# Second feed-forward of a two-layer diffusion backbone: gate and up matmuls with operands in two scaled fp16 parts

## The chip, the cores and the metric

The kernel runs on one NeuronCore of a Trainium2 chip. The time is the device time of one launch in microseconds (us). TensorE (PE in the profile) does matmuls, VectorE (DVE) and ScalarE (ACT) elementwise work, GpSimd (POOL) and SyncE (SP) mostly issue DMA transfers; each engine works through its own instructions in order and waits on semaphores for the others.

## The reference, cut to what matters

Two layers work on 1024 latent tokens and 256 context tokens with 1024 channels. Layer 0 mixes with Fourier and Hyena branches, layer 1 with neighbourhood attention. Each layer ends in a modulated SwiGLU feed-forward of width 2816:

```python
def swiglu(u, w_gate, w_up, w_down):
    return (jax.nn.silu(u @ w_gate) * (u @ w_up)) @ w_down
...
h_lat = h_lat + g2 * swiglu(modulate(rms_norm(h_lat, norm2_g[i]), sh2, sc2),
                            ffn_w_gate[i], ffn_w_up[i], ffn_w_down[i])
```

`sh2`, `sc2` and `g2` are columns per channel, made from the conditioning vector by a matrix product with `ada_w`. All inputs are float32.

## The kernel before

Channels lie on the 128 partitions, tokens along the free dimension. To keep float32 accuracy every operand of a large product is split in two parts: `hi` is the value rounded to fp32r (a reduced float32 that PE takes at a high rate), `lo` is what is left, also in fp32r. A product is three matmuls, hi x hi, hi x lo and lo x hi, into the same PSUM bank. The split is one cast on ScalarE (L349) and one subtraction on VectorE (L351), both in `split`.

The feed-forward `ffn` runs once per layer. Gate and up go through 11 iterations; iteration i takes two rows of 128 output channels of each matrix and computes them by Strassen-Winograd's scheme for 2x2 blocks: seven block products instead of eight. `wino_weights` loads two weight rows of 128x1024, and makes the sums S1 to S4 of their quarters on VectorE (L1866 to L1874) and the split parts of A11, A12, A22 and S1 to S4. `wino_steps` issues the products. A product is 4 blocks x 3 = 12 matmuls of 128x512 (`prod`, L1888), so gate and up of an iteration are 2 x 7 x 12 = 168 and a layer's are 1848. Products that share a PSUM bank follow each other, and ScalarE copies the bank's sum out between them (`snap`, L1893), so that PE may only go on in that bank behind the copy. The other side, the blocks B and T of the normed input (`self.X`, 28 pairs of hi and lo), is made in `wino_first` and `wino_second` (L1779 is a `lo` there). `finish` (L1982 and on) multiplies silu(gate) by up and POOL stores seven blocks for `down`, the third matrix (L2065), which keeps fp32r in both layers.

Between the two layers run `values` (the value projection of layer 1) and the attention. The first layer's stage also computes the modulation columns of layer 1: `ada_group` loads 128x1024 pieces of `ada_w` over the POOL queue (L336 in `ldr`) and reduces them on VectorE (L561), three pieces per iteration. Ahead of layer 1's iterations, `wino_begin` starts five half products (120 matmuls), while the norm of its input is still being worked out (`rms_begin`, with a square root at L604; `rms_end`, L615).

Tiles come from pools with a fixed number of buffers: `S4` (128x1024 float32, 21 buffers), `S2` (128x512, 35), `G` (4), `T`, `TK`, `ws`/`wh`/`wl` for weights. A scheduler that estimates times puts the program's instructions in a fixed order on each engine, and a load into a buffer waits until the buffer's last user is done. `with self.follow(ins)` binds an instruction behind another.

Of the kernel before, what the change touches and what calls it, by code (L numbers as in the profile page):

```python
# [258 lines left out]
class Builder:  # L259
    def __init__(self, ctx, tc, a, out, taps=None, stop=None):  # L260
# [17 lines left out]
        self.banks = 8  # L278
        self.sq = {}

    def pad(self, pool, w):
# [1462 lines left out]
    def pair(self, key, wide):  # L1744

        if wide:
            t = self.S4(F32R)
            t = (t[:, :512], t[:, 512:])
        else:
            t = (self.S2(F32R), self.S2(F32R))  # L1750
        self.X[key] = t
        return t

    def wino_first(self, h, l, m, r):

        nc = self.nc
        self.X, self.raw = {}, {}
        for j in range(4):
            for b in (j, j + 4):
# [4 lines left out]
                nc.scalar.activation(hi, t, AF.Identity, bias=sh)  # L1764
                nc.vector.scalar_tensor_tensor(lo, t, sh, hi.bitcast(F32), op0=ADD, op1=SUB)
                self.raw[b] = t
                yield

    def wino_second(self, h, l, m, r):
# [6 lines left out]
        def out(key, j, src):  # L1776
            hi, lo = self.pair((key, j), l == 1 or len(self.X) < 17)
            nc.scalar.copy(hi, src)
            los.append(nc.vector.tensor_tensor(lo, src, hi.bitcast(F32), SUB).ins)  # L1779

# [42 lines left out]
        for j in range(4):  # L1823
# [3 lines left out]
            nc.scalar.activation(hi, t22, AF.Identity, bias=sh)  # L1827
            nc.vector.scalar_tensor_tensor(lo, t22, sh, hi.bitcast(F32), op0=ADD, op1=SUB)
            yield

    def wino_first_row(self, src, wide):

        wh, wl = self.weights(src, wide=wide)
        return {"A11": (wh[:, :512], wl[:, :512]), "A12": (wh[:, 512:], wl[:, 512:])}

    def wino_weights(self, src, done=None, half=None):

# [14 lines left out]
        w = {} if done is None else done  # L1852
        if done is None:
            wh = self.W("wh", "wh", F32R)
# [4 lines left out]

        def op(key, x):  # L1860
            hi, lo = self.T(F32R) if key == "S4" else self.S2(F32R), self.S2(F32R)
            self.split(x, hi, lo)
            w[key] = (hi, lo)

# [56 lines left out]
    def wino_pair(self, l, i, m, done=None, half=None):  # L1921
        w = self.a[("gate", "up")[m]]
        return self.wino_weights([w[l, 2 * i], w[l, 2 * i + 1]], done, half)

    def wino_begin(self, l, i, m, tile, ctile=None, wide=True):

        w = self.wino_first_row(self.a[("gate", "up")[m]][l, 2 * i], wide)
        s = Steps(self.wino_steps(w, tile, ctile))
# [4 lines left out]
    def ffn(self, l, u, h, hs, second, after, keep=None, begun={}):  # L1933
# [24 lines left out]
        if u is not None:  # L1958
            for fb in range(NFB):
# [10 lines left out]
                if fb >= 2:  # L1970
# [22 lines left out]
        for i in range(NFB // 2):  # L1993
# [20 lines left out]
            for k in (3, 4, 5) if i == 0 and l == 1 else ():  # L2014
                g.to(k)
                up.to(k)
            g.to(5)
            up.to(1)
            g.to(7)
            gate = dict(self.res)  # L2020
            for k in ((0, 0), (1, 1), (0, 1)):
                nc.scalar.activation(gate[k], gate[k], AF.Silu)
            t = self.G()
            nc.scalar.activation(t, gate[(1, 0)], AF.Silu)
# [11 lines left out]
            for _ in range(3 if i < 8 else 2):  # L2036
                next(todo, None)
        prev[0].to(7)
        finish(n2 - 1, prev[1])
# [443 lines left out]
    def run(self):  # L2483
# [372 lines left out]
```

## Time and profile before

| | |
|---|---|
| runs, median of 3 | 2882.15 us (2878.31 to 2882.6) |
| the profiled execution, its span | 2876.0 us |
| its gate and up matmuls of layer 0, starts (L1888) | 902.7 to 1322.8 us |
| its gate and up matmuls of layer 1, starts (L1888) | 2222.9 to 2656.0 us |
| HBM traffic over the span | 183 GB/s |

The profiled execution has a span but no time of its own from outside; the median of the runs is 6.15 us above the span. In the profile, a line such as `L1888 PE MATMUL ps<-s,s 128*128 128x512 f32` names the source line, the engine, the operation, output and inputs, the weights' and the output's shape and the type (fp32r shows as f32 for matmuls). `PEld` is the load of the weights into the array, which overlaps the matmul before. In a timeline, "x30" is a run of 30 such instructions, with the start of the first, the time until the end of the last, and in brackets how long the engine idled before and what released it. A matmul's own duration includes its latency; its rate is read from the number of matmuls in a stretch.

### The profile page before, as it was taken

To read this page: it belongs to the slowest core of one execution; us is meant where nothing else is said; L and a number is where in the kernel's file an instruction comes from. 1 tells how busy PE (TensorE), PEld (TensorE's weight loads), DVE (VectorE), ACT (ScalarE), POOL (GpSimd) and SP (SyncE) were. 2 spreads that over 40 slices of the span, in tenths; PEclk is the share of its full clock that TensorE was granted. 3 is DMA by queue.
4 is the path that set the end of the run, shared out by engine and by line. 5 is a ranking of instruction groups with operands and counts; after the bars stand their busy time and mean duration, and the time that the engine had idled before them with its cause. 6 is when DMAs were issued, how large, how long until landed. Compare 5 with 4: busy or idle time off the path is not lost. (4 is left out here: it accounts for less than half of the span.)

```text
span 2876.0 us, 43758 instructions
## 1 busy us (share of the span) xinstructions
PE 2777.6 (97%) x15570; PEld 2330.9 (81%) x15570; DVE 2089.7 (73%) x3653; ACT 1318.9 (46%) x2267; POOL 539.9 (19%) x873
## 2 busy tenths in 40 slices
PE   7999889999999999999999999999999999999998
PEld 3877677788899888888888888888887788888887
DVE  5678788768777888967777536777777987664556
ACT  3434225543554333333445426777764533333434
POOL 1210234351001112212010002232222022112000
PEclk9999999999999999999999999999999999999999
DMA  7355536756556555659885436777866376434763
GB/s 261 104 161 174 179 117 209 231 171 232 204 184 210 198 198 196 221 183 336 302 307 167 147 116 154 194 180 187 233 211 221 101 254 225 149 110 166 230 195 134
DMA packets 298600, 557.35 MB, mean 194 GB/s; under 512 B 82056, under 2 KB 128842, under 8 KB 298382
## 3 DMA queue, kind: packets, MB, share of 16 engines
q1 hardware_dynamic: 234894, 367.34, 41.2%
q0 software_dynamic: 60640, 182.50, 18.1%
q10 hardware_dynamic: 2848, 4.72, 0.4%
q8 instruction: 123, 2.02, 0.3%
q14 instruction: 95, 0.78, 0.1%
HBM read 407.10 MB, written 119.80 MB: 183 GB/s over the span
## 5 line engine op out<-in xcount | busy, mean ns | idle before, releaser
L1888 PE MATMUL ps<-s,s 128*128 128x512 f32 x1976 | 488.1, 390 | 1.1 <-ACT g L1893 1.1
L1888 PEld LDWEIGHTS ps<-s,s 128*128 128x128 f32 x1976 | 370.9, 188 | 78.9 <-ACT g L1893 1.5
L345 PE MATMUL ps<-s,wh 128*128 128x256 f32 (+1 forms) x1784 | 412.9, 334 | 4.0 <-DVE s L786 1.8
L345 PEld LDWEIGHTS ps<-s,wh 128*128 128x128 f32 x1784 | 299.0, 190 | 39.2 <-DVE s L786 2.3
L345 PE MATMUL ps<-s,wl 128*128 128x256 f32 (+1 forms) x892 | 273.5, 332 | 2.0 <-DVE wl L351 2.0
L349 ACT CAST s<-s 128x1024 fp32r<-128x1024 f32 (+2 forms) x192 | 172.4, 926 | 197.3 <-DMA s<-d 171.5
L2065 PE MATMUL ps<-s,s 128*128 128x512 f32 (+1 forms) x1000 | 259.8, 383 | 3.2 <-DVE s L351 3.1
L351 DVE TENSOR_TENSOR wl<-ws,wh 128x1024 fp32r<-128x1024 f32 (+1 forms) x141 | 168.9, 1200 | 123.8 <-ACT wh L349 119.2
L345 PE MATMUL pq<-s,wh 128*128 128x512 f32 (+1 forms) x840 | 256.1, 385 | 0.6 <-DVE s L897 0.6
L345 PE MATMUL ps<-s,s 128*128 128x65 f16 (+4 forms) x2748 | 229.2, 235 | 16.1 <-DMA s<-tk 9.0
L349 ACT CAST wh<-ws 128x1024 fp32r<-128x1024 f32 (+1 forms) x141 | 144.4, 1026 | 202.3 <-PE ps L345 87.9
L349 ACT CAST s<-t 128x512 fp32r<-128x512 f32 (+2 forms) x238 | 133.9, 583 | 224.6 <-PE ps L1888 76.2
L351 DVE TENSOR_TENSOR s<-s,s 128x1024 fp32r<-128x1024 f32 (+2 forms) x170 | 190.6, 1154 | 58.2 <-ACT s L349 58.0
L2065 PEld LDWEIGHTS ps<-s,s 128*128 128x128 f32 x1000 | 184.5, 188 | 41.2 <-DVE s L351 4.9
L351 DVE TENSOR_TENSOR s<-t,s 128x512 fp32r<-128x512 f32 (+2 forms) x238 | 150.9, 649 | 76.7 <-ACT s L349 57.4
L1888 PE MATMUL ps<-s,wh 128*128 128x512 f32 x616 | 191.5, 390 | 0.0
L345 PEld LDWEIGHTS ps<-s,wl 128*128 128x128 f32 x892 | 167.9, 191 | 20.1 <-DVE wl L351 3.2
L336 POOL DMA_DIRECT2D d<-s x186 | 101.0, 544 | 368.1 <-DVE s L1695 94.2
L345 PEld LDWEIGHTS pq<-s,wh 128*128 128x128 f32 x840 | 149.8, 189 | 22.6 <-DVE s L897 1.0
L345 PE MATMUL pq<-s,wl 128*128 128x512 f32 (+1 forms) x420 | 159.4, 379 | 0.0
L2065 PE MATMUL ps<-s 128*128 128x512 f32 (+1 forms) x500 | 150.9, 385 | 0.0
L345 PEld LDWEIGHTS ps<-s,s 128*128 128x128 f32 (+1 forms) x828 | 130.0, 193 | 24.2 <-issue 2.8
(493 smaller groups left out, 5554.7 us busy)
## 6 DMA issues: line engine op xcount, KB each, us to landing
s<-d SPq DMA_DIRECT2D x283, 256.0 KB, 4.0
d<-s POOLq DMA_DIRECT2D x170, 256.0 KB, 4.0
s<-in_down SPq DMA_DIRECT2D x150, 256.0 KB, 4.3
s<-in_ada_w POOLq DMA_DIRECT2D x64, 512.0 KB, 4.8
ws<-in_up SPq DMA_DIRECT2D x44, 512.0 KB, 3.6
d<-g POOLq DMA_DIRECT2D x86, 256.0 KB, 3.0
ws<-in_gate SPq DMA_DIRECT2D x42, 512.0 KB, 3.6
d<-tk POOLq DMA_DIRECT2D x66, 256.0 KB, 4.4
```

The source lines that it names most:

```text
L336: self.last_ldr = self.nc.gpsimd.dma_start(out, in_).ins
L345: self.last_mm = self.nc.tensor.matmul(o, l, r, start=st, stop=sp).ins
L349: self.last_hi = nc.scalar.copy(hi, src).ins
L351: self.last_lo = eng.tensor_tensor(lo, src, hi.bitcast(F32), SUB).ins
L1888: nc.tensor.matmul(ps, x[:, sl], y, start=first and j == 0 and x is wh and y is xh, stop=j == 3 and x is wl, skip_group_check=True)
L2065: m = nc.tensor.matmul(acc[j][:, c0:c1], x[:, sl], y[:, xs], start=first and k == 0, stop=last and k == 2, skip_group_check=True)
```

## The change

In layer 1's gate and up, both parts of every operand become fp16. fp16 has a small range, so both sides are scaled first. The weights get one scale per matrix: during layer 0's iterations 1 to 10, `scan` loads all 44 rows of layer 1's gate and up once more (512 KB each, POOL queue, into `S4`) and ScalarE sums the absolute values of each row (`Abs` with an accumulator). `scale_w` takes the largest sum over partitions (one `partition_all_reduce` on POOL) and per matrix, and makes the scale and, with the input's, its inverse. `scale_x` bounds the normed input from its modulation columns (another `partition_all_reduce`) and scales these columns, so the input comes out scaled. The gate's inverse goes into Silu's `scale`, the up's into the column `g2`.

`split_scaled` makes the weight parts: `hi` by an activation with the scale column, `lo` by a scalar_tensor_tensor. Both lie side by side in one tile: an fp16 tile `hl` of 128x2048 in a `wh` or `wl` buffer for a first row (one buffer where two were used), an `S2` tile of 128x1024 for each other one (one instead of two). The X parts lie four to an `S4` tile. Matmul count and shapes stay as they are.

```diff
     def pair(self, key, wide):
-        if wide:
+        if self.f16:
+            if self.two is None:
+                self.two = self.S4(F16, 2048)
+                t = self.two[:, :1024]
+            else:
+                t, self.two = self.two[:, 1024:], None
+            t = (t[:, :512], t[:, 512:])
+        elif wide:
...
+    def scale_x(self, l, m):
+        nc = self.nc
+        ad = self.ada[(l, 0)]
+        t, r = self.C(2), self.C(2)
+        nc.vector.tensor_reduce(t[:, 0:1], ad[:, m * 8:m * 8 + 8], axis=AX, op=MAX, apply_absolute_value=True)
+        nc.vector.tensor_reduce(t[:, 1:2], ad[:, m * 8 + 8:m * 8 + 16], axis=AX, op=MAX, apply_absolute_value=True)
+        nc.gpsimd.partition_all_reduce(r, t, channels=P, reduce_op=bass.bass_isa.ReduceOp.max)
+        nc.vector.scalar_tensor_tensor(t[:, 0:1], r[:, 1:2], 32.0, r[:, 0:1], op0=MUL, op1=ADD)
+        nc.vector.tensor_scalar(t[:, 0:1], t[:, 0:1], 1e-30, 1.0 / 8192.0, op0=MAX, op1=MUL)
+        nc.vector.reciprocal(t[:, 1:2], t[:, 0:1])
+        nc.vector.tensor_scalar(ad[:, m * 8:m * 8 + 16], ad[:, m * 8:m * 8 + 16], t[:, 1:2], None, op0=MUL)
+        self.xinv = t[:, 0:1]
+    def scan(self, key, tiles):
...
+        for k in range(n + 2):
+            if k < n:
+                t = self.S4()
+                self.ldr(t, tiles[k])
+                st.append(t)
+            if k > 1:
+                t = st.pop(0)
+                nc.scalar.activation(t, t, AF.Abs, accum_out=sums[:, k - 2:k - 1])
+            yield
+        self.wsc[key] = sums
+    def scale_w(self, key, groups):
...
+        nc.gpsimd.partition_all_reduce(sums[:, n:], sums[:, :n], channels=P, reduce_op=bass.bass_isa.ReduceOp.max)
+        for j, k in enumerate(groups):
...
+            nc.vector.tensor_reduce(s, sums[:, n + j * w:n + j * w + w], axis=AX, op=MAX)
+            nc.vector.tensor_scalar(s, s, 1e-30, 1.0 / 8192.0, op0=MAX, op1=MUL)
+            nc.vector.tensor_tensor(inv, s, self.xinv, MUL)
+            nc.vector.reciprocal(s, s)
+            self.wsc[k] = s, inv
+    def split_scaled(self, src, t, s):
+        w = src.shape[1]
+        hi, lo = t[:, :w], t[:, w:2 * w]
+        self.last_hi = self.nc.scalar.activation(hi, src, AF.Copy, scale=s).ins
+        self.last_lo = self.nc.vector.scalar_tensor_tensor(lo, src, s, hi, op0=MUL, op1=SUB).ins
+        return hi, lo
...
-        def op(key, x):
-            hi, lo = self.T(F32R) if key == "S4" else self.S2(F32R), self.S2(F32R)
+        def op(name, x):
+            if key is not None:
+                w[name] = self.split_scaled(x, self.S2(F16, 1024), s)
+                return
+            hi, lo = self.T(F32R) if name == "S4" else self.S2(F32R), self.S2(F32R)
...
+        ahead = iter(())
+        if l == 0:
+            ahead = self.scan("next", [a[x][1, fb] for x in ("gate", "up") for fb in range(NFB)])
...
+            if i:
+                next(ahead, None)
             g.to(5)
             up.to(1)
+            if i:
+                next(ahead, None)
             g.to(7)
             gate = dict(self.res)
+            inv = self.wsc[(l, 0)][1] if l in self.half else 1.0
             for k in ((0, 0), (1, 1), (0, 1)):
-                nc.scalar.activation(gate[k], gate[k], AF.Silu)
+                nc.scalar.activation(gate[k], gate[k], AF.Silu, scale=inv)
...
+            if i:
+                next(ahead, None)
             up.to(5)
+            if i:
+                next(ahead, None)
...
+        self.half.add(1)
+        self.scale_x(1, 3)
+        self.scale_w("next", [(1, 0), (1, 1)])
+        ad = self.ada[(1, 0)]
+        nc.vector.tensor_scalar(ad[:, 40:48], ad[:, 40:48], self.wsc[(1, 1)][1], None, op0=MUL)
         for i, _ in enumerate(self.values(u1)):
```

The scheduler lays the new work between the old. First place, an iteration of layer 0: POOL's queue before, with its loads of `ada_w` (into `s`) among the stores of `finish` (from `g`, `tk`) and of the sums for `down` (from `s`).

```order
L336 DMA d_7404<-g_9748 128x512
L336 DMA s_2658_10659<-in_ada_w 128x1024
L336 DMA d_7406<-tk_9980 128x512
L336 DMA s_2663_10669<-in_ada_w 128x1024
L336 DMA d_7475<-s_2587_10314 128x512
L336 DMA d_7477<-s_2586_10313 128x512
```

And the same place of POOL's queue in the changed kernel (lines are numbered two higher there).

```order
L338 DMA d_7404<-g_9759 128x512
L338 DMA s_2657_10521<-in_gate 128x1024
L338 DMA d_7406<-tk_10000 128x512
L338 DMA s_2664_10595<-in_gate 128x1024
L338 DMA s_2666_10628<-in_gate 128x1024
L338 DMA s_2671_10687<-in_gate 128x1024
L338 DMA d_7475<-s_2601_10349 128x512
L338 DMA d_7477<-s_2600_10348 128x512
L338 DMA d_7476<-s_2602_10350 128x512
L338 DMA s_2676_10706<-in_ada_w 128x1024
L338 DMA s_2681_10716<-in_ada_w 128x1024
```

Four scan loads stand where two of `ada_w` stood, and these two come behind the three stores. ScalarE in the same iteration, before: casts of the weight parts, copies of PSUM sums (`g` of the gate, `tk` of the up), Silu.

```order
L2022 ACTIVATE g_10078<-g_10078 128x512
L349 CAST s_2571_10147<-ws_10122 128x512
L1893 COPY g_10195<-ps_10065 128x512
L1893 COPY tk_10296<-ps_10212 128x512
L1893 COPY g_10209<-ps_10065 128x512
L349 CAST s_2611_10371<-t_10368 128x512
```

And in the changed kernel, where L1810 is the scan's pass and L1980 the copy.

```order
L2119 ACTIVATE g_10101<-g_10101 128x512
L351 CAST s_2581_10170<-ws_10145 128x512
L1810 ACTIVATE s_2657_10521,c_9496<-s_2657_10521 128x1024
L1980 COPY g_10221<-ps_10088 128x512
L1980 COPY tk_10328<-ps_10238 128x512
L1810 ACTIVATE s_2664_10595,c_9496<-s_2664_10595 128x1024
L1810 ACTIVATE s_2666_10628,c_9496<-s_2666_10628 128x1024
L1980 COPY g_10235<-ps_10088 128x512
L351 CAST s_2625_10406<-t_10403 128x512
```

Three passes now stand among the copies, one ahead of the first and two ahead of the third. Second place, the start of layer 1's gate and up: ScalarE before, with the copy of the first product, the root of the norm (L604, into `st`) and the first Silu.

```order
L1893 COPY g_23699<-pq_23686 128x512
L604 ACTIVATE st_23720<-ps_23715,c_93 128x4
L2022 ACT_TABLE_LOAD
L2022 ACTIVATE g_23699<-g_23699 128x512
L615 ACTIVATE t_23758<-c_86,st_23720 128x128 x4
```

And in the changed kernel (L1834 is a scaled weight part, L606 the root, L617 the former L615).

```order
L1980 COPY g_23839<-pq_23826 128x512
L1834 ACTIVATE hl_23975<-s_5054_23973,c_15381 128x1024
L2119 ACT_TABLE_LOAD
L2119 ACTIVATE g_23839<-g_23839,c_15381 128x512
L606 ACT_TABLE_LOAD
L606 ACTIVATE st_23860<-ps_23855,c_93 128x4
L617 ACTIVATE t_23897<-c_86,st_23860 128x128 x4
```

The Silu moved ahead of the root, and a table load stands before each. Third place, PE in layer 1's first product of the gate; before, the weights are `wh` and `wl`, X is `s`.

```order
L1888 MATMUL pq_23686<-s_4904_23340,wh_23681 128x512 x2
L1888 MATMUL pq_23686<-s_4904_23340,wl_23682 128x512
L1888 MATMUL pq_23686<-s_4913_23378,wh_23681 128x512 x2
L1888 MATMUL pq_23686<-s_4913_23378,wl_23682 128x512
L1888 MATMUL pq_23686<-s_4922_23416,wh_23681 128x512
```

And in the changed kernel, where both parts of the weights lie in `hl`.

```order
L1975 LDWEIGHTS hl_23823
L1975 MATMUL pq_23826<-s_4958_23494,hl_23823 128x512
L1975 LDWEIGHTS hl_23823
L1975 MATMUL pq_23826<-s_4958_23494,hl_23823 128x512
L1975 LDWEIGHTS hl_23823
L1975 MATMUL ps_23841<-s_4958_23494,hl_23823 128x512
```

Each fp16 weight load is a row of its own now, while an fp32r matmul is printed together with its weight load; and a second product (bank `ps_23841`) is mixed into the first.

More of the change, by code (lines that the diff above doesn't have):

```diff
@@ L279, in __init__ @@
         self.sq = {}
+        self.half = set()
+        self.wsc = {}
     def pad(self, pool, w):
@@ L2037, in ffn @@
                 next(todo, None)
+        for _ in ahead:
+            pass
         prev[0].to(7)
```

50 lines of the change are left out of this document (39 added, 11 removed).

## The prediction

> **What bounds the kernel now.** I read the page's busy shares first, then the granted clock, then the stages in windows, and last what TensorE waited for at the one line that the change is about.
>
> ```profile
> span 2876.0 us, 43758 instructions
> PE 2777.6 (97%) x15570; PEld 2330.9 (81%) x15570; DVE 2089.7 (73%) x3653; ACT 1318.9 (46%) x2267; POOL 539.9 (19%) x873
> PEclk9999999999999999999999999999999999999999
> ```
>
> TensorE (PE) is busy for 97% of the span at the full clock, so only what shortens its work, or what makes it wait, moves the time. A busy PE is not yet a PE at its best rate, so the windows come next: one inside the second feed-forward's gate and up, one inside the first's, and the two whole stages for L1888 alone (the matmuls of the gate and up products).
>
> ```profile
> core 0: us, PE busy (x) PEld busy (x) DVE busy (x) ACT busy (x) POOL busy (x), PEclk, DMA share, GB/s
> 2300.00:2500.00 200.00, 200.00 (x884) 165.71 (x883) 152.62 (x233) 73.84 (x122) 42.09 (x78) 1.00 0.62 214
> 1050.00:1100.00 50.00, 50.00 (x223) 41.41 (x222) 42.39 (x80) 18.82 (x30) 9.18 (x17) 1.00 0.58 191
> ...
> 902.50:1323.50 421.00, 419.39 (x1848) 347.02 (x1848) 1.00 0.61 209
> 2222.50:2657.00 434.50, 421.48 (x1848) 346.61 (x1848) 1.00 0.48 168
> ```
>
> The second stage holds 1848 matmuls (11 iterations of 168), each 128x512. From 2300 to 2500 nothing else runs on PE, and 200.0 us / 884 = 0.2262 us from one to the next. 1848 x 0.2262 = 418.0 us, of a stage 434.5 long that also holds some other matmuls. The list of what PE waited for at this line, both stages together, confirms it:
>
> ```profile
> its engine sat idle before it (us, times) until:
>   DVE s L1779: 4.6, 2
>   ACT g L1893: 2.5, 2
>   ACT wh L349: 2.2, 2
> ```
>
> About 10 us in 837: both stages are bound by the rate at which PE takes fp32r matmuls, not by weights, vector work or transfers.
>
> **The change part by part.** *The rate.* All 1848 matmuls of the second stage get fp16 operands; their number and shape stay (the order of the changed kernel has 1848 matmuls with 1848 separate weight loads there). No 512-column fp16 matmul is in this trace, so the price is bounded by three rows: fp16 matmuls of the attention, their weight loads, and plain f32 matmuls of 512 columns.
>
> ```profile
> 1776.82 1.08 PE L345 MATMUL ps<-s,s 128*128 128x65 f16 x30
> L345 PEld LDWEIGHTS <-s 128*128 128x128 f16 x1920 | 67.1, 98 | 12.3 <-DMA s<-tk 10.1 <-issue 1.3
> 33.76 0.59 PE L519 MATMUL ps<-s,c 128*2 128x512 f32 x1
> 34.75 5.31 PE L519 MATMUL ps<-s,c 128*2 128x512 f32 x12 [0.40 <-DMA s<-in_ada_k]
> ```
>
> Thirty fp16 matmuls of 64 or 65 columns, each with its own weight load, take 1.08 us; without the last one's latency (0.19) that is 0.0306 us each, so an fp16 weight load (0.098 long) hides even behind 65 columns and will hide behind 512. The plain f32 row gives (5.31 - 0.59) / 11 = 0.429 us for 512 columns at full clock; I read it as two passes of 0.2146, which is how fast the array takes 512 columns when fp32r does not slow it. Extending the fp16 row by 447 columns gives 0.218 at that slope (0.000419 per column), and 0.228 at fp32r's own slope (0.2262 / 512). So the ends are 0.2146 and 0.228. I take **0.216**, nearest to the plain f32 row, because that row has the same 512 columns, with half of the fp16 row's fixed part (0.0306 - 65 x 0.000419 = 0.003) on top. Saving: (0.2262 - 0.216) x 1848 = **18.8 us**; by the lower end 21.4, by the upper none.
>
> The Trainium skill (TensorE: Matmul & The Clock Gate, Back-to-back issue gap) has N / 2.4 + 2.5 ns for warm bf16 matmuls, 215.8 ns at 512 columns; by it the saving would be 10.4 ns x 1848 = 19.2 us. The fp32r row, 226.2, does not follow that formula, so the trace itself leaves open whether fp16 does.
>
> *ScalarE and VectorE in that stage.* Each split now scales by a column of a tile. In the stretch before the stage, both kinds stand side by side:
>
> ```profile
> 2208.25 0.72 ACT L1764 ACTIVATE s<-s,c 128x512 fp32r<-128x512 f32 x1
> ...
> 2210.42 0.61 ACT L349 CAST s<-g 128x512 fp32r<-128x512 f32 x1
> 2209.52 0.75 DVE L1765 SCALAR_TENSOR_TENSOR s<-s,c,s 128x512 fp32r<-128x512 f32 x1
> ...
> 2212.64 0.69 DVE L351 TENSOR_TENSOR s<-g,s 128x512 fp32r<-128x512 f32 x1
> ```
>
> Twelve splits and four Silus per iteration cost ScalarE 16 x 0.11 = 1.8 us more, and VectorE 12 x 0.06 = 0.7. An iteration takes 168 x 0.2262 = 38.0 us and will take 36.3. VectorE is busy 152.62 of 200, or 29.0 per iteration; 29.7 of 36.3 is 82%. ScalarE goes from 14.0 to 15.8. PE hides both: 0. If that cover went, the price would be those 2.5 us per iteration.
>
> *The scan in the first stage.* 44 loads of 512 KB join the POOL queue, and 44 passes with a sum join ScalarE, from the second iteration on. The like of such a pass is L659 (with its accumulator read), the like of such a load the one of in_ada_w, here between 950 and 1290:
>
> ```profile
> L659 ACT ACTIVATE t<-s x5: 1039/1056/1057, 22.2 to 35.0; 128x1024 bf16<-128x1024 f32 x5
> L659 ACT ACTIVATION_READ_ACCUMULATOR t<-s x5: 185/186/187, 23.1 to 36.0; 128x1 f32 x5
> DMA to landing us min/median/max: 3.7/4.4/6.0
> ```
>
> ScalarE gets 4.4 x 1.24 = 5.5 us per iteration beside 18.82 of 50: room enough. DMA gets 2.3 MB per 38 us, 61 GB/s on 191. The narrow place is elsewhere: of the pool's 21 buffers 17 hold X parts and two the conditioning, so two are left for seven loads per iteration (three of in_ada_w, four of the scan). The tighter buffer passes through four loads, three passes and one reduction: 4 x 4.4 + 3 x 1.24 + about 3 = 24 us of 38. That fits, but ScalarE works in order, and the passes stand ahead of PSUM copies that PE waits for. Here are the reductions that free the buffers, and those copies:
>
> ```profile
> 1033.23 0.74 DVE L561 CUSTOM_DVE_ANT_0 s<-s,s,ah 128x512 f32<-128x512 f32 x1
> ...
> 1040.07 0.74 DVE L561 CUSTOM_DVE_ANT_0 s<-s,s,ah 128x512 f32<-128x512 f32 x1
> 1037.61 0.59 ACT L1893 COPY g<-ps 128x512 f32<-128x512 f32 x1 [3.64 <-PE ps L1888]
> ...
> 1045.31 0.59 ACT L1893 COPY g<-ps 128x512 f32<-128x512 f32 x1 [5.76 <-PE ps L1888]
> ```
>
> A scan load issued at 1034.3 lands at 1038.7, its pass ends at 1039.9; the next, in the same buffer, lands at 1044.6 and ends at 1045.9; the third (other buffer, free at 1041) ends at 1047.1. The first copy is 2.3 us late and the second ends at 1047.7. By PE's order 18 matmuls (4.1 us) stand between the product that the second copy reads and the next one into that bank, so it must end by 1049.4: 1.7 us to spare. I take 1 us in all; bounds 0 and 10 (1 us per iteration, landings of 5.75).
>
> *The scale.* Two reductions across partitions run on POOL, and VectorE waits for one of them inside the first down projection, in front of weight splits of that stage:
>
> ```profile
> L2228 POOL PARTITION_ALL_REDUCE c<-c x1: 1380/1380/1380, 1714.6 to 1714.6; - x1
> 1330.00:1380.00 50.00, 50.00 (x222) 41.41 (x221) 29.40 (x46) 16.85 (x16) 4.77 (x9) 1.00 0.83 293
> 1430.00:1480.00 50.00, 50.00 (x222) 41.45 (x221) 35.12 (x57) 21.20 (x30) 14.33 (x27) 1.00 0.90 312
> ```
>
> 1.4 us of wait and some twelve operations on one column: 3 us once, on an engine that idles 15 to 20 of 50 there. 0; bounds 0 and 3.
>
> *The start of the second stage.* In the changed order ScalarE runs a Silu ahead of the root of the norm (it came behind it), and so loads tables twice more.
>
> ```profile
> 2230.97 0.26 ACT L604 ACTIVATE st<-ps,c 128x4 f32<-128x4 f32 x1 [1.12 <-PE ps L345]
> 2231.25 1.28 ACT L2022 ACT_TABLE_LOAD   x1
> 2232.55 0.63 ACT L2022 ACTIVATE g<-g 128x512 f32<-128x512 f32 x1
> 2233.09 1.27 ACT L615 ACTIVATE t<-c,st 128x128 f32<-128x128 f32 x4
> 2230.55 0.69 DVE L1902 TENSOR_TENSOR g<-ps,g 128x512 f32<-128x512 f32 x1
> ```
>
> Silu now comes at 2231.2, then 1.28 for the table, the root and its reciprocal: L615 starts near 2233.6 instead of 2233.1. The 120 matmuls begun ahead get 1.2 us shorter, and a second table switch costs up to 1.3 among the splits of X, so PE's wait for L1779 may grow by 3. Against that, one weight tile instead of two per begun product can take away the 1.1 us waits for L349. I take +1.5; bounds -1.1 and +3.
>
> *Sum.* -18.8 + 1 + 0 + 1.5 = -16.3 us on this execution's 2876.0. The runs' median is 2882.15, 6.15 above that span; I carry the difference over: **2866 us** (0.6% faster).
>
> **The rivals.** *Width is not what costs.* If the 0.2262 comes from something that fp16 shares, the stage keeps its 418 us and only the 2.5 us of cost remain: 2884.7 us. For it: 0.0306 us for 65 columns is 0.00047 per column, no better than fp32r's 0.00044, so the rows don't show that fp16 streams faster. Against it: the plain f32 row streams faster on the same array and clock. The Trainium skill (TensorE: Matmul & The Clock Gate, Weight-path perf modes) speaks for this rival: a narrower operand streams no faster, since the array takes one element per cell and cycle whatever its width. The trace before has no 512 columns in 16 bits to test it.
>
> *The scan holds ScalarE's queue (the slower side).* Two loads follow each other through one buffer ahead of the second copy, so each microsecond of later landing makes that copy 2 us later; past 5.25 us the 1.7 us are used up and PE stands still in each of the ten iterations. To end slower by over 0.2% it must eat 18.8 - 1.5 and 5.8 more, 2.3 us per iteration, which needs landings of 6.4 us. At 7 us: 3.5 x 10 - 17.3, so 2900 us. For it: the scan adds a third to the DMA traffic, and the largest landing is 6.0 already. Against it: the median is 4.4 at a DMA share of 0.58, and the share would be about 0.77, still below the 0.83 to 0.90 at which the first down stage keeps PE at 222 matmuls per 50 us.
>
> **How the numbers follow.** The forecast has 0.83 (0.02 of it with costs so high that it ends above 2876.4), unchanged width 0.11, the held queue 0.06. About 0.2% (5.8 us) is what a measurement of this kernel can tell from no change, so faster means below 2876.4: 0.81 of the forecast; within 0.2% lie the first rival and the forecast's rest, 0.13; slower is the second rival, 0.06. The range takes the bounds: at the low end 0.2146 per matmul and the gain at the start, 2882.15 - 21.4 - 1.1 = 2859.7, less 2.5 since the runs shown scatter by 4; at the high end 0.218 (-15.2) with 10 + 3 + 3 of costs, 2883, cut to 2882 as not all bounds fall together. That leaves out both rivals, 0.17.
>
> **What would show it.** Right: some 925 L1975 matmuls in 200 us of the second stage (0.216 apart), a stage near 417 us instead of 434.5, and a first stage still within 2 us of 421. The rate is wrong if they stay 0.226 apart. The scan is wrong if PE idles before matmuls of the first stage until the copies of L1980 (the L1893 of now), or landings of in_gate on the POOL queue exceed 5.3 us. The start is wrong if PE's wait for L1848 (the L1779 of now) is far from 5 us. What would overturn the whole is VectorE becoming the releaser throughout the second stage.

## The result, and the profile after

The changed kernel takes **2910.56 us** (median of 4 runs, 2904.16 to 2912.86) against 2880.23 us of the kernel before on the same chip: ratio 1.0104, 95% interval 1.0083 to 1.0124. It is 1.0% slower, where 0.6% faster was forecast. First the page of its profiled execution (busy time and share by engine, then PE over 40 slices).

```profile
span 2911.1 us, 43904 instructions
PE 2777.9 (95%) x15570; PEld 2174.7 (75%) x15570; DVE 2090.4 (72%) x3668; ACT 1379.6 (47%) x2357; POOL 564.4 (19%) x919
PE   7999888999999999999999999999999989999998
```

PE is busy as long as before although 1848 matmuls got shorter, and two slices of 72.8 us have an 8 where a 9 stood before: from 437 us, ahead of the first gate and up, and from 2329 us, early in the second. By stage (worked out from the starts of the gate and up matmuls and of the attention's first and last row sums; "output projection" reaches from the last row sum to the first L1975 matmul of layer 1):

| us | before | after | difference |
|---|---|---|---|
| up to the first gate and up | 902.7 | 907.7 | +5.0 |
| first gate and up | 420.0 | 436.0 | +16.0 |
| first down, values, until the attention's first row sum | 438.5 | 439.6 | +1.1 |
| attention | 395.5 | 405.0 | +9.5 |
| output projection | 66.1 | 71.6 | +5.5 |
| second gate and up, to the end | 653.0 | 651.2 | -1.8 |

The faster matmuls are worth 18.8 us in the last row and 1.8 arrive, so 17 are lost there.

**The rate came as forecast.** In windows of the second gate and up of the changed kernel, one late and two early (columns as in the prediction's windows):

```profile
2470.00:2670.00 200.00, 200.00 (x929) 90.66 (x927) 99.39 (x141) 66.40 (x97) 31.03 (x57) 1.00 0.35 115
...
2299.90:2339.90 40.00, 35.42 (x162) 15.51 (x160) 40.00 (x63) 22.51 (x36) 4.89 (x9) 1.00 0.54 176
2339.90:2379.90 40.00, 36.33 (x160) 16.08 (x161) 40.00 (x63) 19.80 (x29) 10.85 (x20) 0.96 0.93 334
```

Late in the stage 929 matmuls stand in 200 us (forecast: some 925), 0.216 us from one start to the next by the median. That is also what the formula for a lone gap in the Trainium skill gives (TensorE: Matmul & The Clock Gate, Back-to-back issue gap), 215.8 ns; the 131 ns that the same section has for a stream of weight loads and matmuls did not come, though such a stream ran here. The Trainium skill's section on weight-path modes, the source of the first rival, does not cover what fp32r cost here. But early in the stage PE runs 160 to 162 in 40 us, fewer than the 176 to 178 of before, and VectorE is busy without a gap. The same places before:

```profile
2262.90:2302.90 40.00, 39.92 (x176) 32.71 (x176) 36.49 (x60) 18.43 (x32) 6.48 (x12) 1.00 0.55 190
2302.90:2342.90 40.00, 40.00 (x178) 33.16 (x177) 35.68 (x56) 17.65 (x32) 9.71 (x18) 1.00 0.74 261
```

VectorE was at 90% there already; the prediction's window (2300 to 2500, 76%) lay mostly behind it. What PE waited for at L1975, first in the first stage, then in the second (us, times):

```profile
  ACT g L1980: 22.7, 17
  ACT tk L1980: 2.6, 2
  DVE g L1999: 1.6, 2
...
  issue: 19.2, 32
  DVE s L1835: 11.4, 5
  ACT g L1980: 8.9, 4
  ACT s L1834: 3.2, 2
```

The list can count a wait at a weight load and again at the matmul behind it, so its times are longer than what PE lost; nearly all of `issue` stands at weight loads. The matmuls alone stood idle 11.0 us in the first stage, 9.0 of them for ScalarE's copies out of PSUM (L1980 into `g`), and 17.5 in the second: 8.9 for copies again, 5.0 for VectorE's low parts of weights (L1835), 1.4 for high parts (L1834). Before, it was 0.0 and 4.2 (the prediction's 10 us are such a list too). Three timelines show how. The end of the first stage, VectorE, then POOL, then ScalarE:

```profile
1271.52 0.69 DVE L353 TENSOR_TENSOR s<-t,s 128x512 fp32r<-128x512 f32 x1
1276.98 0.18 DVE L1824 TENSOR_REDUCE c<-c 128x1 f32<-128x22 f32 x1 [4.78 <-POOL c L1819]
1277.08 0.68 DVE L2074 TENSOR_TENSOR g<-tk,g 128x512 f32<-128x512 f32 x1
...
1269.13 0.55 POOL L338 DMA_DIRECT2D d<-g  x1 [4.86 <-DVE g L2074]
1276.43 0.52 POOL L1819 PARTITION_ALL_REDUCE c<-c  x1 [6.75 <-issue]
1278.06 0.74 POOL L338 DMA_DIRECT2D d<-g  x1 [1.11 <-DVE c L1824]
...
1280.62 0.59 ACT L1980 COPY g<-ps 128x512 f32<-128x512 f32 x1 [7.86 <-DMA d<-g]
```

POOL stands still for 6.75 us ahead of the reduction over the scan's sums, and only in the first 1.0 us of it for something that the profile shows (the last of these sums). VectorE's next instruction waits for that reduction; the product that fills a `g` buffer (L2074) is queued behind it, its store behind that. ScalarE's next copy waits 7.86 us for a `g` buffer, and PE loses 3.9 us, from one matmul's start to the next, to that copy. Then the second stage, 153 us after its start (VectorE, POOL, ScalarE and PE together; L2036 to L2039 are the sums for `down`):

```profile
2413.01 0.68 DVE L2039 TENSOR_TENSOR s<-s,s 128x512 f32<-128x512 f32 x1
...
2415.54 0.68 DVE L2074 TENSOR_TENSOR g<-tk,g 128x512 f32<-128x512 f32 x1
...
2416.51 0.54 POOL L338 DMA_DIRECT2D d<-g  x1 [1.98 <-DVE g L2074]
2416.74 0.68 DVE L2036 TENSOR_TENSOR s<-s,s 128x512 f32<-128x512 f32 x1
...
2422.23 0.59 ACT L1980 COPY g<-ps 128x512 f32<-128x512 f32 x1 [1.66 <-DMA d<-g]
...
2422.87 2.72 PE L1975 MATMUL ps<-s,s 128*128 128x512 f16 x6 [4.52 <-ACT g L1980]
```

VectorE works without a gap, and sums stand among the splits and the products that fill `g` buffers (L2074). A copy waits until such a buffer is stored, and PE 4.52 us for the copy. From 40 to 165 us of the stage, 37 operations of the sums and 60 low parts of weights stand on VectorE; before, 24 and 50. The output projection, VectorE:

```profile
2220.11 1.82 DVE L353 TENSOR_TENSOR wl<-ws,wh 128x768 fp32r<-128x768 f32 x2
2221.85 5.38 DVE L1773 SCALAR_TENSOR_TENSOR s<-s,c,t 128x512 f32<-128x512 f32 x8
2227.15 2.07 DVE L1835 SCALAR_TENSOR_TENSOR s<-t,c,s 128x512 f16<-128x512 f32 x3
...
2233.77 0.95 DVE L353 TENSOR_TENSOR wl<-ws,wh 128x768 fp32r<-128x768 f32 x1
```

Between two low parts of `w_out2` (L353), which PE needs at once, stand eight products for the next stage's input and several weight splits of it. PE stood idle 3.17 us for the second of them (at 2234.8), and the clock was half for 6.8 us from 2233.0. Before, five such products stood there and the next low part came 7.7 us after the last, not 13.7:

```profile
2188.89 1.82 DVE L351 TENSOR_TENSOR wl<-ws,wh 128x768 fp32r<-128x768 f32 x2
2190.63 3.40 DVE L1762 SCALAR_TENSOR_TENSOR s<-s,c,t 128x512 f32<-128x512 f32 x5
...
2196.59 0.95 DVE L351 TENSOR_TENSOR wl<-ws,wh 128x768 fp32r<-128x768 f32 x1
```

What lets them in is room, as the runs of buffers below show: the 28 pairs of X lay in 20 large and 16 small buffers and now lie in 14 large ones, and each weight split takes one buffer instead of two.

### The profile page after: what moved, and what is told of

Read it like the earlier page. It is cut to its first block, busy times and chain, and to the rows that moved or that the text cites. A ratio compares the mean times of both kernels' runs of the same rounds, so it can differ in the third digit from the quotient of the medians.

```text
span 2911.1 us, 43904 instructions
## 1 busy us (share of the span) xinstructions
PE 2777.9 (95%) x15570; PEld 2174.7 (75%) x15570; DVE 2090.4 (72%) x3668; ACT 1379.6 (47%) x2357; POOL 564.4 (19%) x919
## 5 line engine op out<-in xcount | busy, mean ns | idle before, releaser
L1975 PE MATMUL ps<-s,s 128*128 128x512 f32 (+1 forms) x2104 | 504.9, 388 | 24.1 <-ACT g L1980 17.5
L2168 PE MATMUL ps<-s,s 128*128 128x512 f32 (+1 forms) x1000 | 260.0, 383 | 3.4 <-DVE s L353 3.3
L1975 PEld LDWEIGHTS <-s 128*128 128x128 f16 x1320 | 129.7, 99 | 178.0 <-issue 18.6
L1975 PEld LDWEIGHTS ps<-s,s 128*128 128x128 f32 x1144 | 214.8, 189 | 59.6 <-ACT g L1980 13.7
L347 PE MATMUL ps<-s,s 128*128 128x65 f16 (+4 forms) x2748 | 231.1, 236 | 21.4 <-DMA s<-tk 10.4
L353 DVE TENSOR_TENSOR wl<-ws,wh 128x1024 fp32r<-128x1024 f32 (+1 forms) x124 | 148.2, 1197 | 122.6 <-ACT wh L351 117.9
L353 DVE TENSOR_TENSOR s<-s,s 128x1024 fp32r<-128x1024 f32 (+2 forms) x170 | 190.8, 1154 | 62.6 <-ACT s L351 56.0
L2168 PEld LDWEIGHTS ps<-s,s 128*128 128x128 f32 x1000 | 184.5, 188 | 41.4 <-DVE s L353 4.8
L351 ACT CAST wh<-ws 128x1024 fp32r<-128x1024 f32 (+1 forms) x124 | 126.7, 1023 | 186.7 <-PE ps L347 97.1
L351 ACT CAST s<-t 128x512 fp32r<-128x512 f32 (+2 forms) x172 | 93.3, 566 | 114.8 <-DVE t L689 18.7
L353 DVE TENSOR_TENSOR s<-t,s 128x512 fp32r<-128x512 f32 (+2 forms) x172 | 106.4, 634 | 26.7 <-ACT s L351 24.2
```

Source lines behind the costliest of these rows:

```text
L347: self.last_mm = self.nc.tensor.matmul(o, l, r, start=st, stop=sp).ins
L351: self.last_hi = nc.scalar.copy(hi, src).ins
L353: self.last_lo = eng.tensor_tensor(lo, src, hi.bitcast(F32), SUB).ins
L1975: nc.tensor.matmul(ps, x[:, sl], y, start=first and j == 0 and x is wh and y is xh, stop=j == 3 and x is wl, skip_group_check=True)
L2168: m = nc.tensor.matmul(acc[j][:, c0:c1], x[:, sl], y[:, xs], start=first and k == 0, stop=last and k == 2, skip_group_check=True)
```

## The experiments

All at once, so that they can be compared (stages as above, from one profiled execution each; ratios to the kernel before, from medians of 4 to 12 runs each). How far a stage scatters can be read off: five kernels whose edits leave the second stage alone (after, no_scan, narrow_pass, late_red, red_x) lie between 651.0 and 651.7 us in it.

| run | ratio [95%] | first gate and up | output projection | second gate and up to the end |
|---|---|---|---|---|
| before | 1 | 420.0 | 66.1 | 653.0 |
| after | 1.0104 [1.0083, 1.0124] | 436.0 | 71.6 | 651.2 |
| no_scan | 1.0046 [1.0031, 1.0062] | 420.0 | 72.3 | 651.4 |
| scan_only | 1.0031 [1.0016, 1.0047] | 432.4 | 65.4 | 654.9 |
| narrow_pass | 1.0041 [1.0026, 1.0056] | 426.4 | 72.0 | 651.7 |
| late_red | 1.0082 [1.0060, 1.0103] | 436.4 | 71.4 | 651.0 |
| red_x | 1.0050 [1.0032, 1.0068] | 432.8 | 71.4 | 651.2 |
| spread_sums | 1.0064 [1.0043, 1.0086] | 441.3 | 71.0 | 647.6 |
| sums_no_dve | 1.0026 [1.0012, 1.0041] | 439.6 | 71.1 | 635.9 |
| late_sums | 1.0045 [1.0029, 1.0061] | 436.9 | 71.1 | 638.3 |
| old_all | 1.0045 [1.0026, 1.0064] | 440.6 | 63.9 | 646.5 |
| old_x | 1.0052 [1.0034, 1.0071] | 436.0 | 64.8 | 644.8 |
| old_parts | 1.0046 [1.0025, 1.0067] | 439.6 | 72.0 | 639.7 |
| old_const | 0.9998 [0.9986, 1.0010] | 420.0 | 65.7 | 646.3 |
| best_x | 0.9976 [0.9962, 0.9991] | 427.6 | 65.5 | 643.6 |
| best2 | 0.9968 [0.9955, 0.9980] | 423.2 | 65.3 | 645.3 |
| best3 | 0.9965 [0.9950, 0.9981] | 422.9 | 65.9 | 642.9 |
| best2c | 0.9991 [0.9973, 1.0008] | 420.0 | 66.0 | 644.3 |

### The first stage: the scan

no_scan:

```diff
-            ahead = self.scan("next", [...])
+            self.wsc["next"] = self.C(88)
+            nc.gpsimd.memset(self.wsc["next"], 28.0)
```

> The 44 loads and 44 passes of the scan go; the sums that they would have given are one constant, set once (28 for each weight tile), and everything behind them stays. Theory 2 (loads and passes of the scan make PE wait in the first gate and up stage): that stage goes from 436.2 us to 420 to 425 (the upper end if the wait of POOL ahead of its reduction across partitions, 6.75 us, stays in it), and the time falls by 11 to 16 us to 2894 to 2900, with the second stage still near 431. Rival (the first stage is longer for another reason, such as the clock of that run): it stays over 430. The values and attention stage stays near 635 us if its 15 us come from the order of the scaled splits, and falls to 620 if they come from the scan or from chance.

The first stage is back at 420.0, the other two stay: all 16 us there are the scan and what hangs on it, and neither other loss is. (With constant sums their reduction moved to 15 us after the start, so this run does not part it from the scan.)

scan_only leaves out the lines in `run` from `self.half.add(1)` to the scaling of the `g2` columns.

> The scan runs, its sums are not used: no reductions across partitions, no scales, and the second feed-forward keeps its fp32r parts. Theory 2: the first gate and up stage is still 428 to 436 us (4 to 6 us less than 436 for the missing reduction on POOL), all later stages are as in the kernel before (620 for values and attention, 433 for the second gate and up), and the time is 2888 to 2896. Rival (the scan fits into the idle time, as predicted, and the loss comes from the fp16 half of the change): first stage within 3 us of 420, time within 4 us of the kernel before.

432.4 us, with all of layer 1 as before: loads and passes alone cost 12.4 us.

narrow_pass:

```diff
-                nc.scalar.activation(t, t, AF.Abs, ...
+                nc.scalar.activation(t[:, :1], t[:, :1], AF.Abs, ...
```

> Each pass of the scan reads one column instead of 1024, so its 1.05 us on ScalarE become about 0.2; loads, buffers and waits stay. The scales then come from one column of each weight tile. If the length of the passes is what delays the copies of L1980, the first gate and up stage falls from 436 us to 422 to 428 and the time by 8 to 14 us. If it is the waiting of ScalarE for the landings, the loads that stand ahead of the stores in POOL's queue, or the reduction on POOL, the stage stays at 432 to 437 and the time within 5 us of the changed kernel.

426.4 us. What ScalarE waited for ahead of the passes, changed kernel, then this one (us, times):

```profile
  DMA s<-in_gate: 36.7, 14
  DMA s<-in_up: 24.5, 13
...
  DMA s<-in_gate: 49.1, 14
  DMA s<-in_up: 41.4, 18
```

It waits longer for landings than before, 90 us against 61, and yet PE has one wait left over 1.5 us in the stage, the 4.6 us at the reduction. Nor did the scan's loads land sooner: after 5.5 (gate) and 5.8 us (up) by the median, against 5.2 and 5.4. So it is the passes' own length, 44 x 1.24 us in ScalarE's order, that makes the copies late, not the landings.

late_red put the scale chain under `with self.follow(self.last_mm)`.

> The scale chain (both reductions across partitions and what follows them) may only start behind the last matmul of the first down projection; the scan stays as it is. Theory: POOL stands 6.75 us ahead of the reduction, in the last iteration of the first gate and up stage, with the stores that free the g buffers behind it in its queue, and PE waits 3.9 us and then runs half-clocked for 3.4; without it the first stage falls from 436 us (436 to 441 in the runs with the whole scan) to 430 to 434, no wait of over 2.5 us is left in it, and nothing else moves. Rival: the late store comes from the scan loads in POOL's queue, and the wait near the stage's end stays at 3 to 4 us.

It tested nothing: the binding holds only for instructions on that matmul's own engine, and every engine's order came out as in the changed kernel. It is a repeat of that: 1.0082, with 903.9 us up to the first gate and up (907.7) and 391.1 in the attention (405.0). red_x binds on POOL:

```diff
+        with self.follow(self.x_red):
+            self.scale_w("next", [(1, 0), (1, 1)])
-        self.scale_w("next", [(1, 0), (1, 1)])
```

(`x_red` is the reduction in `scale_x`, which stands in the first down projection.)

> The reduction of the scan's sums is queued behind the other one on POOL, so that it stands in the first down projection (in the run before it the edit did not move it); the scan stays whole. Theory: the reduction near the end of the first gate and up stage (POOL 6.8 us ahead of it, VectorE 5 us behind it, then the stores of g) costs that stage 4 us of wait and 1.7 of half clock, so the stage falls from 436 to 441 us to 430 to 435 and the waits left in it are those of ScalarE's passes, each under 2.5 us. Rival (the scan's loads and passes alone delay the last stores): the wait of 4 us stays and the stage at 436 to 441.

432.8 us, and no wait over 1.9 us left. The eight runs with whole scan and early reduction average 438.3 (436.0 to 441.3), the two without that reduction 432.6, the one with it and short passes 426.4. So the scan costs 12.6 without its reduction, the reduction 5.7, and 11.9 go with the length of the passes.

### The second stage and the output projection: room for work ahead

spread_sums asks for one group of down weights per iteration:

```diff
-            for k in (2 * i - 2, 2 * i - 1) if l == 1 else (9, 10) if i == 9 ...
+            for k in (9, 10) if i == 9 ...
```

> One line: in the second feed-forward the sums of the down weights are asked for one pair per iteration (as in the first one), not two. Theory 1 (the scaled parts need fewer small buffers, so the loads and sums of the down weights run ahead, fill VectorE, 40.00 us of 40 from 2302 to 2422, and PE waits for splits and copies): the busy share of VectorE there falls under 37 of 40, the second gate and up stage goes from 431.5 us to 416 to 420, and the time falls by 11 to 15 us against the changed kernel, to about 2897. Rival (the fp16 splits themselves come late, because of their scale columns or their shared buffers): the stage stays within 3 us of 431 and the time at 2907 to 2914.

The expectations of this part speak of the stage up to its last gate or up matmul. That is 433.1 us before, 431.5 after, 422.7 in spread_sums, 426.6 in old_all, 419.9 in old_x, 414.0 in old_parts, 413.1 in late_sums and 426.3 in old_const. But in spread_sums, old_x, old_parts and late_sums 22 matmuls of `down`, 5.0 us, stand behind that last matmul, where the others have them ahead of it. Hence the table goes to the end.

So spread_sums gains 8.8 us up to that matmul, but to the end 3.6 of the 17 come back, far from the theory's 11 to 15. (Its median is some 11 us below the changed kernel's all the same; in the profiled executions the attention is 10.8 us shorter, which the edit does not touch.) VectorE stays full, with 68 low parts of weights from 40 to 165 us of the stage (60 in the changed kernel, 50 before). When one kind of work is held back, another comes ahead.

The three runs of buffers:

> The fp16 parts lie in as many buffers of the same pools as the fp32r parts did (X parts: one large or two small ones a pair; weight parts: high and low in a buffer each); all else is the changed kernel. Theory 1 (freed buffers let splits and sums of later weights run ahead in VectorE's order): split subtractions of weights from 40 to 165 us of the second gate and up stage go back from 60 to 50 or 52, VectorE is no longer at 40.00 of 40 there, the stage falls from 431.5 us to 415 to 420, the output projection with the start ahead of it from 71.6 to 65 to 67, and the ratio to the kernel before from 1.0104 to 1.003 to 1.005. Rival (the scaled fp16 split itself, 0.83 us instead of 0.80, or its place is what fills VectorE): VectorE stays full, the stage at 428 to 434, the ratio over 1.008.

> Only the X parts go back to the buffers of before (20 large and 16 small ones instead of 12 large ones); weight parts stay two in a buffer. If the 16 freed small buffers are what lets later work run ahead, the second gate and up stage falls to 416 to 422 us and the output projection stays at 71 to 72. If it is the weight parts, the stage stays at 428 to 433.

> Only the weight parts go back to the buffers of before (a buffer each for high and low, two pairs of the large ones instead of four); the X parts stay four to a buffer. If the first rows of four begun products, split ahead of the last splits of w_out2, are what delays the output projection, it falls from 71.6 us to 65 to 67; the second stage stays at 426 to 433 if the X parts are what counts there, and falls to 416 to 422 if the weight parts are.

(There are 14 large ones, not the 12 that the second expectation names.) The X parts' old buffers cure the output projection (64.8), the weight parts' do not (72.0): the expectations had it the other way round there. In the second stage each gives a part back, 6.4 us (old_x) and 11.5 (old_parts), and both together no more than 4.7 (old_all). Yet old_all has VectorE's order as the theory wanted it: from 40 to 165 us 24 operations of the sums and 47 low parts, and VectorE at 28.7 to 37.9 of 40. PE still stands idle 15.2 us in the stage, 8.6 of them for copies. So the freed buffers do bring the work ahead, which explains the output projection; in the second stage it is not all, and why both together give less than either stays open.

sums_no_dve leaves out the four vector operations of `sums` in layer 1:

> In the second feed-forward the four vector operations on each group of down weights (44 in all, 30 us of VectorE) are left out: the weights are loaded and stored as they are, so the second down projection works on other sums. Theory 1b (VectorE cannot feed PE in the first 160 us of the stage, at 97% of each shortened iteration): from the stage's first matmul to the end, 651.3 us in the changed kernel, falls by 10 to 16 us, and VectorE is no longer full from 40 to 160 us. Rival (order or transfers, such as the stores that free g buffers at a DMA share of 0.9): it falls by less than 5 us.

late_sums only moves them:

```diff
-            for k in (2 * i - 2, 2 * i - 1) if l == 1 else ...
+            for k in (2 * i - 10, 2 * i - 9) if l == 1 else ...
```

> The sums of the down weights start in the sixth iteration of the second gate and up stage (two groups an iteration until the last), where VectorE is idle for a third of the time, instead of the second; nothing is left out. Theory 1b: the waits of PE in the stage fall from 19 us to under 8, and from the stage's first matmul to the end 636 to 642 us instead of 651.3, as much as the sums without vector work give. Rival (later weight splits run ahead in their place and VectorE is as full as in the kernel with one group an iteration): 646 to 650 us.

635.9 and 638.3 us: 15 and 13 of the 17 us are there again. sums_no_dve keeps all loads and stores (the DMA share reaches 1.03 in it too), so it is the vector operations that cost, not the transfers; VectorE is at 39.6 and 40.0 of 40 until 120 us all the same. In late_sums the matmuls stand idle 8.4 us instead of 17.5. Two windows of it, from 80 us of the stage on:

```profile
2328.10:2368.10 40.00, 38.36 (x177) 17.15 (x176) 39.99 (x61) 25.45 (x41) 5.94 (x11) 1.00 0.56 186
2368.10:2408.10 40.00, 40.00 (x187) 18.14 (x186) 40.00 (x63) 19.45 (x30) 9.21 (x17) 1.00 0.80 267
```

VectorE is as full as in the changed kernel, and PE takes 177 and 187 matmuls instead of 160 and 164. So a full VectorE does not by itself hold PE (and in old_all one that is not full does not free it). What the two runs leave is the order, what stands ahead of PE's next operand: splits of later weights are PE's own next work, sums for the third matrix are not. That reading is argued, no run moves one single operation.

### Versions

old_const (old_all without the scan) should show the rate alone:

> As old_all, with the scan left out (its sums are one constant, 28) and the reductions across partitions put behind the last matmul of the first down projection. If the three costs found so far (16 us of the scan and its reduction in the first stage, 14 in the second stage, 5.5 in the output projection) are all there is, what is left is the gain of the rate: first stage 420 us, output projection 65 to 67, second stage 415 to 420, and a ratio to the kernel before of 0.994 to 0.996. If the rate of fp16 is worth less than 14 us in the whole program, the ratio is over 0.997.

0.9998, where 0.994 to 0.996 was expected. The second stage gave back too little, as in old_all, so the run does not show the rate alone. And the three stages gain 7.1 us in sum, which would be 0.9975, below the interval: some 6 us are lost outside them in the median of ten runs (see the end of the next section). best_x and best2 keep a scale from the data, though from an eighth of each weight row, which does not bound the rest:

```diff
-                self.ldr(t, tiles[k])
-                st.append(t)
+                self.ldr(t[:, :128], tiles[k][:, :128])
+                st.append(t[:, :128])
```

> Four edits together: the scan reads 128 of the 1024 columns of each weight tile (loads of 64 KB, short passes), the reductions stand behind the last matmul of the first down projection, the X parts lie in the buffers of before, and the sums start in the sixth iteration. If the costs found add up: first gate and up stage 420 to 422 us, output projection 65, from the second stage's first matmul to the end 634 to 641 us instead of 653.1 in the kernel before, and a ratio to that of 0.993 to 0.997. If the second stage is held by the order of its work whatever the buffers and sums, it is 644 to 647 us and the ratio 0.997 to 1.001.

In best_x the reduction stayed in the first stage (its edit was late_red's), so 427.6; the second stage came out at 643.6, nearer to the rival's 644 to 647 than to the sum of the cures. best2 has red_x and late_sums, the change's own buffers, and

```diff
             if i > 12 and i % 3 == 1:
-                next(first, None)
+                with self.follow(self.last_lo):
+                    next(first, None)
...
-        drain(self.wino_pair(1, 0, 0, sums, self.G))
+        with self.follow(self.last_lo):
+            drain(self.wino_pair(1, 0, 0, sums, self.G))
```

> The changed kernel's buffers, with four edits: the scan reads 128 of 1024 columns of each weight tile, the reductions stand in the first down projection, the sums start in the sixth iteration of the second stage, and the vector work that prepares the second stage is queued behind the last split of w_out2 asked for ahead of it. If each loss found has its cure: first gate and up stage 420 to 423 us, output projection 65 to 67 (71 to 72 with the free buffers unpaced), from the second stage's first matmul to the end 636 to 640 us, and a ratio to the kernel before of 0.993 to 0.996. If pacing only moves the waits of the output projection into the second stage, that is 643 us or more and the ratio 0.996 to 0.999.

> As best2, with high and low weight parts in a buffer each as before. If less work ahead in VectorE's order is worth something beyond the late sums, the second stage to the end falls 2 to 4 us below best2; if the two cure the same waits, it is within 2 us of it, or longer by the waits for buffers.

> As best2, with the scan left out (its sums are one constant, 28). What the thin scan still costs is the difference: if DMA and ScalarE hide it, the first stage is 420 us in both and the ratios are within 0.001; if its waits on landings hold ScalarE's queue, this one is faster by 2 to 5 us in the first stage.

best2 is **faster than the kernel before by 0.3%** (interval 0.2% to 0.45%), best3 the same within the intervals. Ratio and second stage of best2 lie where its expectation's rival had them. Pacing gave the output projection its 6 us back and took 7 in the second stage (638.3 to 645.3): those waits moved. The thin scan costs 3 us (423.2 against 420.0). best2c's ratio lies above best2's though its three stages are 3.5 us shorter in sum; its attention took 404.8 us in the profile, best2's 390.6.

## Why the prediction was wrong

**The rate** was right: 0.216 us a matmul, so -18.8 us. It was chosen between 0.2146 and 0.228; that it fits to the last digit is in part luck. The rival of unchanged width fell with it.

**ScalarE and VectorE in the second stage** failed: "PE hides both: 0". VectorE's work grew about as forecast (its instructions in the stage sum to 334 us before and 341 after, 0.6 per iteration), but the 152.62 of 200 was an average over a stretch whose first 40 us were at 35 to 36 of 40. And only instructions were counted, not where they stand: buffers that the halved parts free bring sums of the down weights and later splits ahead, between PE and its operands. The stage loses 17 of the 18.8 us: the matmuls stand idle 13.3 us more than before, and the clock is half for 10.2 us, before for none. 13 of the 17 come back when the sums alone go later (8.4 us idle, no half clock); the other 4 are waits that are left, 8.4 against 4.2. How much of the 17 the freed buffers cost is not shown: putting all of them back returns 4.7. What the prediction named as overturning the whole, VectorE as releaser, came in part: 5.0 us of waits for its low parts, and 7.0 for copies that wait for a `g` buffer, stored behind a product of VectorE, all in the stage's first 163 us.

**The scan** was mis-sized: 1 us with an upper bound of 10, measured 12.6. The place was right, copies of L1980 late behind passes, but the sum followed two copies through one iteration by the timing of the landings, and the length of the passes makes 11.9 of the 12.6. The rival had the mechanism, ScalarE's queue held, and made it decide by landings past 5.25 us: the scan's loads landed after 5.2 and 5.4 us by the median, and with short passes after 5.5 and 5.8, with no wait left but the reduction's.

**The scale** failed outright: the wait inside the first down projection was priced, 1.4 us, and the other reduction, which the order puts into the last iteration of the first stage, was not; it costs 5.7 us.

**The start** was wrong in its place: PE's waits for L1848 sank from 4.6 us to 0.2 in that list, but the output projection just ahead of it, which no step looked at, lost 5.5 us by vector work that came ahead into free buffers.

Measured terms, the first two as means over runs: 12.6 + 5.7 + 5.5 - 1.8 = 22 us, a ratio of 1.0076. The repeat in late_red has that within its interval; the changed kernel's own run lies 2 us or more above. The 5.0 us ahead of the first stage and the 9.5 in the attention are not in this sum: over all profiled executions the first varies from 902.6 to 912.5 us, the second from 389.3 to 405.5, and late_red has 391.1 with the very order of the changed kernel. With a long attention go PE's waits for landings of transposed tiles (`s<-tk`, by DMA): 10.4 us in the changed kernel and 15.7 in no_scan (405.5), 5.0 in late_red and 3.0 in best2 (390.6). Why these land late stays open. It may not be scatter alone: in the three kernels without a scan (no_scan, old_const, best2c) the medians of ten runs lie 6 to 9 us above what the three stages give.

## What to carry to other kernels

A change that makes operands smaller also frees buffers, and a scheduler fills them with work that stands in the in-order queues ahead of what the critical engine needs next: compare the order of the feeding engines, not only their load, and give such work a place by hand. Judge whether an engine "hides" more work in the busiest stretch of the stage, not over its mean. Work added on an engine whose short copies release PE costs by its length in that queue, and one rare cross-partition reduction costs by what is queued behind it.

## What the runs showed of the hardware

A wait of PE costs more than itself. After the 3.9 us at the end of the changed kernel's first stage (second column of numbers PE busy with its matmuls, then the granted clock after POOL's):

```profile
1280.70:1284.10 3.40, 2.84 (x7) 2.27 (x8) 3.40 (x6) 2.59 (x4) 1.60 (x3) 0.50 0.71 269
1284.10:1288.00 3.90, 3.90 (x19) 3.21 (x18) 2.91 (x5) 0.59 (x1) 0.00 (x0) 1.00 0.33 86
```

the clock is half for 3.4 us, in which 7 matmuls run, against 19 in the 3.9 us behind it. In the gate and up stages of all profiled executions, 27 of 29 waits over 2.9 us have such a stretch of 3.4 or 6.8 us beside them, and 11 of 77 waits of 1.5 to 2.9 us (a wait here is the time between the starts of two matmuls, less the usual 0.216 or 0.226). The Trainium skill (TensorE: Matmul & The Clock Gate, What's actually happening) has the gate close after an idle window of about 3.4 us that runs freely; here 10 of the 11 waits of 2.9 to 3.4 us have a half-clocked stretch beside them too.

The reduction across partitions itself takes 0.52 us, but POOL stood 6.75 us ahead of it (6.8 in late_red), and its transfers with it; in the changed kernel 1.0 us of that went until the last sum was there. The second one, at 1445, started 0.1 us behind the value that it waits for, with POOL idle for 12 us before. In red_x both stand there, the second right behind the first. Whether a like time lies hidden in those 12 us the runs don't show.
